# Attention probabilities divided by their sums in place on ScalarE, instead of dividing the output, in a hybrid decoder layer

## The chip, the core and the metric

The kernel runs on one core of a Trainium2 chip. TensorE multiplies matrices and transposes through PSUM; VectorE and ScalarE work on tiles in SBUF and PSUM; GpSimd does elementwise work and starts some transfers; SyncE starts most transfers. Each of these engines takes its instructions in the order in which the program gives them, and they meet at semaphores. The metric is the device time of one execution in microseconds (us). 6 us are about 1% of it.

## The reference, cut to what matters

One layer: a projection feeds eight heads of block-sparse attention (at 512 tokens and blocks of 256 each query sees its own block and all earlier ones, so it is causal attention with a bias by distance) and eight heads of a gated recurrence in chunks; both go through one output projection, and an MLP follows. The change is in the softmax.

```python
        l_own = jnp.einsum('bhqd,bhkd->bhqk', qc, k_own).astype(jnp.float32) * scale
        l_own = l_own + rel_bias[:, rel_bucket(d_own)]
        ...
        logits = jnp.concatenate(
            [l_own, l_sel.reshape(B, H, MOBA_QCHUNK, kk * MOBA_BLOCK)], axis=-1)
        p = jax.nn.softmax(logits, axis=-1)
        ...
        return (jnp.einsum('bhqk,bhkd->bhqd', p_own, v_own)
                + jnp.einsum('bhqnk,bhqnkd->bhqd', p_sel, v_sel))
```

## The kernel before, in words

Every matrix product in float32 is done as three products of rounded halves (`mm3`: high by high, high by low, low by high), or as one slow float32 product. The layer is written as generators ("streams"): `projections`, `chunks`, `inverse` and `scan` (the recurrence), `scores` and `values` (the attention), `finish_o`, `weights_out`, `output` and others. A class `Weave` runs them against a clock of TensorE's work: a stream yields a delay or the name of a mark, and the stream of lowest rank whose time has come writes its next piece of code. So the delays, in the tables `WAIT` (by kind of step) and `SINGLE` (for the n-th step of a kind), set TensorE's order: where a stream waits, units of the projections (one `mm3` of 512 columns, three matmuls `ps_mm<-hT...`) fill the gap. The order on the other engines is set by the framework's scheduler up to the MLP; in the MLP it is the order of the code.

Heads go in four pairs p. `scores` makes for each pair four row blocks q = 3, 2, 1, 0 of 128 queries, 128(q+1) keys wide: six matmuls from `pt` into two PSUM banks `ps_a` (one for each head; the tag "a" has three banks), then for each head an addition of the bias with the row's minimum on VectorE (L708, out `L`, `mins`), and the exponential with its sum on ScalarE (L710, out `L`, `sums`). `values` transposes the rows, a block of 128 keys at a time (`ident,L`, eight for k = 0), ScalarE copies them to `ph` (L736), and `product` multiplies them by the values (`ph,V`) into a bank `po`. At the end of a pair the reciprocal of the eight columns of sums is taken (L713), spread by ScalarE over 512 columns (`R`, L715), transposed by TensorE into a further bank (`ident,R`), copied out by ScalarE (`t`, L762) and multiplied into the output by VectorE (L766), which is then split into `ma_h` and `ma_l`.

Meanwhile the recurrence runs on the same engines: `uap` and `UT` are ScalarE's copies between two small products of the inverse (L815, L828), `kB` and `LWQ` follow, and then eight steps of the scan, each with a copy `vn` on ScalarE (L887) between TensorE's `S,LWQ` and `vn,kdec`. The scan's output of each tile (`ot`) is transposed, multiplied by the gate `zs` (`om`, L933) and split into `mg_h`, `mg_l`. The output projection `output` needs `mg_h`, `mg_l` and its weights `wo_h`, `wo_l`, cast on ScalarE (L142) and VectorE (L143) from loads `wo_raw` that share two slots with the last input weights `w_raw`.

Of the kernel before, what the change touches and what calls it, by code (L numbers as in the profile page):

```python
# [16 lines left out]
DRAM = bass.MemoryType.DRAM  # L17
EPS = 1e-6

WAIT = {'h': 1.7, 'conv_k': 5.5, 'k': 5.19, 'conv_q': 6.15, 'q': 2.1, 'conv_v': 11.0, 'v': 6.02, 'z': 2.87, 'ab': 0.1, 'g': 11.93, 'scalars': 4.76, 'r_in': 0.65, 'r_out': 4.45, 'kk': 2.71, 'kk_out': 14.43, 'gl': 3.13, 'qk': 3.88, 'va': 0.83, 'a': 5.81, 'row': 1.38, 'rows': 5.12, 'pv': 1.54, 'att': 1.17, 'inverse': 1.23, 'merge': 11.0, 'p1': 2.8, 'p2': 1.7, 'w': 2.33, 'vn': 1.0, 'state': 1.21, 'o_in': 3.96, 'o': 3.73, 'wo': 0.97, 'wo_out': 17.6, 'normed3': 7.6, 'normed': 11.21, 'n': 1.7, 'up': 1.9, 'sums': 2.64, 'turned': 0.5, 'pv0': 1.53}  # L20

SINGLE = {('h', 0): 0.05, ('inverse', 6): 2.02, ('state', 6): 3.71, ('row', 5): 0.98, ('inverse', 18): 0.05, ('inverse', 25): 0.05, ('vn', 7): 0.05, ('pv', 2): 0.1, ('h', 1): 0.05, ('turned', 0): 0.9, ('conv_k', 0): 4.12, ('normed', 0): 10.21, ('wo', 1): 1.97, ('conv_q', 0): 8.0, ('inverse', 16): 1.63, ('state', 1): 1.57, ('row', 6): 0.38, ('conv_v', 1): 8.5, ('conv_q', 2): 7.0, ('conv_k', 1): 5.1, ('o_in', 1): 4.36, ('kk', 2): 2.03, ('h', 2): 0.85, ('rows', 2): 6.66, ('vn', 1): 0.75, ('pv', 4): 2.77, ('inverse', 0): 0.61, ('rows', 0): 5.52, ('pv', 6): 2.0, ('rows', 4): 0.1, ('conv_v', 0): 14.3, ('kk_out', 0): 11.93, ('gl', 0): 5.63, ('inverse', 27): 0.23, ('row', 12): 2.48, ('state', 0): 0.21}

RANK = {'chunks': 1, 'inverse': 3, 'scan': 3, 'scores': 5, 'values': 5, 'finish_o': 2, 'take': 4}
LEAD = {'chunks': 0, 'inverse': 100, 'scan': 100, 'scores': 0, 'values': 100, 'finish_o': 0, 'take': 200, 'take_a': 100}
# [60 lines left out]
def layer(ctx, tc, nc, x, w_in, w_v, w_ab, w_out, w_up, w_down, conv_w, a_log, dt_bias, gdn_norm_w, rel_bias,  # L86
# [588 lines left out]

    rows_of, sums_of = {}, {}


    def scores():
        for p in range(4):
            yield f"a{p}"
            if p:
                yield f"turned{p - 1}"
            T = [pts[p][:, i] for i in range(4)]
            Es = []
            for hh in range(2):
                E = at.tile([128, 512], FT, name="E")  # L690
                nc.sync.dma_start(E, bass.AP(tensor=d_e.tensor, offset=d_e.offset + 640 * (2 * p + hh), ap=[[1, 128], [1, 512]]))
                Es.append(E)
            Ls = [at.tile([128, 1280], FT, name="L") for _ in range(2)]
            mins = at.tile([128, 4, 2], FT, name="mins")
            sums = at.tile([128, 4, 2], FT, name="sums")
            for q in (3, 2, 1, 0):
                w = 128 * q + 128
                qs = slice(128 * q, 128 * q + 128)
                s = [bank("a") for _ in range(2)]
                for n, (i, j) in enumerate(((0, 2), (0, 3), (1, 2))):  # L700
                    for hh in range(2):
                        hs = slice(64 * hh, 64 * hh + 64)
# [15 lines left out]
    def values():  # L720
        for p in range(4):
# [646 lines left out]
    rs = {}  # L1368
# [165 lines left out]
```

## Time and profile before

| | |
|---|---|
| median of three runs | 633.07 us (632.63 to 636.78) |
| the profiled execution | 636.12 us |
| its span, first to last instruction | 634.2 us |
| busy: TensorE, VectorE, ScalarE, GpSimd | 622.9, 443.7, 359.4, 157.9 us |
| granted TensorE clock, mean | 0.998 |

The profile is of one execution. Matmuls overlap: one of 512 columns is listed with 0.39 us, and the next starts 0.23 us behind it, so what a group of matmuls costs is read from its start to the start of the next one. An idle time in brackets stands ahead of the instruction that waited, with the instruction that released it.

### The profile page before, as it was taken

To read this page: it belongs to the slowest core of one execution; us is meant where nothing else is said; L and a number is where in the kernel's file an instruction comes from. 1 tells how busy PE (TensorE), PEld (TensorE's weight loads), DVE (VectorE), ACT (ScalarE), POOL (GpSimd) and SP (SyncE) were. 2 spreads that over 40 slices of the span, in tenths; PEclk is the share of its full clock that TensorE was granted. 3 is DMA by queue.
4 is the path that set the end of the run, shared out by engine and by line. 5 is a ranking of instruction groups with operands and counts; after the bars stand their busy time and mean duration, and the time that the engine had idled before them with its cause. 6 is when DMAs were issued, how large, how long until landed. Compare 5 with 4: busy or idle time off the path is not lost.

```text
span 634.2 us, 11129 instructions
## 1 busy us (share of the span) xinstructions
PE 622.9 (98%) x4359; PEld 524.1 (83%) x4359; DVE 443.7 (70%) x635; ACT 359.4 (57%) x610; POOL 157.9 (25%) x197
## 2 busy tenths in 40 slices
PE   8999999999999999999999999999999999999995
PEld 6877777877876777688998999999998888888884
DVE  4456667599724464658665678878789888887776
ACT  6366586254387548654225586566765656665661
POOL 4346555500234343004212311111130320000001
PEclk9999999999999999999999999999999999999999
DMA  7222332422731112563488899999999999867503
GB/s 247 78 90 83 84 109 76 128 88 71 186 94 52 36 35 82 188 229 132 162 336 233 159 276 268 228 241 286 270 264 340 310 291 285 270 213 283 198 1 132
DMA packets 60629, 113.16 MB, mean 178 GB/s; under 512 B 15734, under 2 KB 35321, under 8 KB 60194
## 3 DMA queue, kind: packets, MB, share of 16 engines
q1 hardware_dynamic: 42876, 83.09, 37.8%
q0 software_dynamic: 17696, 29.36, 22.2%
q8 instruction: 34, 0.56, 0.3%
q14 instruction: 17, 0.14, 0.1%
q10 hardware_dynamic: 6, 0.00, 0.0%
HBM read 106.65 MB, written 35.15 MB: 224 GB/s over the span
## 4 chain that ended last, share of the span: by engine, by line
PE 91%; DVE 3%; DMA 2%; ACT 2%; POOL 1%; issue 0%; POOLq 0%; DVEq 0%; SPq 0%; ACTq 0%
PE ps_mm L97 46%; PE ps_g L97 26%; PE ps_a L97 16%; PE ps_a L101 2%; PE ps_g L101 1%; DMA wo_raw<-in_w_out 1%; DMA xx<-in_x 1%; DVE conv L412 1%; DMA w_raw<-in_w_in 0%; DVE wo_l L143 0%; POOL w_lo L155 0%; POOL oss L192 0%; DVE hT_l L131 0%; POOL by L192 0%; DVE xs L249 0%
## 5 line engine op out<-in xcount | busy, mean ns | idle before, releaser
L130 ACT CAST wdh<-wd 128x1024 fp32r<-128x1024 f32 x53 | 55.9, 1054 | 51.4 <-PE ps_mm L97 22.6
L131 DVE TENSOR_TENSOR u_l<-w,u_h 128x1024 fp32r<-128x1024 f32 x46 | 56.2, 1224 | 37.3 <-ACT u_h L130 37.1
L131 DVE TENSOR_TENSOR wdl<-wd,wdh 128x1024 fp32r<-128x1024 f32 x53 | 64.9, 1224 | 22.2 <-ACT wdh L130 22.1
L130 ACT CAST u_h<-w 128x1024 fp32r<-128x1024 f32 x46 | 47.9, 1046 | 56.8 <-DVE w L1177 15.6
L97 PE MATMUL ps_mm<-hT_h,w_hi 128*128 128x512 f32 (+1 forms) x192 | 79.4, 413 | 0.0
L97 PE MATMUL ps_mm<-hT_l,w_hi 128*128 128x512 f32 (+1 forms) x192 | 74.6, 388 | 0.3 <-DVE hT_l L131 0.3
L97 PE MATMUL ps_mm<-hT_h,w_lo 128*128 128x512 f32 (+1 forms) x192 | 74.5, 388 | 0.0
L155 POOL TENSOR_TENSOR w_lo<-w_raw,w_hi 128x512 fp32r<-128x512 f32 x40 | 51.8, 1297 | 77.2 <-ACT w_hi L154 67.4
L1210 POOL DMA_DIRECT2D d_T<-in_w_down x32 | 33.0, 1033 | 143.8 <-DMA d_T<-in_w_down 82.4
L154 ACT CAST w_hi<-w_raw 128x512 fp32r<-128x512 f32 x56 | 34.6, 620 | 52.9 <-PE ps_mm L97 17.5
L97 PEld LDWEIGHTS ps_mm<-hT_h,w_hi 128*128 128x128 f32 x192 | 37.1, 193 | 11.3 <-issue 4.8
L97 PE MATMUL ps_mm<-wdh,u_h 128*128 128x512 f32 x116 | 45.2, 390 | 0.0
L97 PE MATMUL ps_mm<-wdl,u_h 128*128 128x512 f32 x116 | 45.1, 389 | 0.0
L97 PE MATMUL ps_mm<-wdh,u_l 128*128 128x512 f32 x116 | 45.1, 389 | 0.0
L97 PEld LDWEIGHTS ps_mm<-hT_h,w_lo 128*128 128x128 f32 x192 | 37.2, 194 | 7.5
L97 PEld LDWEIGHTS ps_mm<-hT_l,w_hi 128*128 128x128 f32 x192 | 37.3, 194 | 6.0 <-DVE hT_l L131 0.6
L412 DVE SCALAR_TENSOR_TENSOR conv<-ps_mm,cw,conv 128x511 f32<-128x511 f32 (+2 forms) x36 | 26.8, 745 | 11.3 <-ACT conv L409 11.0
L131 DVE TENSOR_TENSOR u_l<-f,u_h 128x1024 fp32r<-128x1024 f32 x28 | 34.1, 1217 | 0.0
L708 DVE CUSTOM_DVE_ANT_0 L<-ps_a,E 128x512 f32<-128x512 f32 (+3 forms) x32 | 14.4, 489 | 23.9 <-PE ps_a L97 23.7
L97 PE MATMUL ps_g<-wdh,u_h 128*128 128x512 f32 x80 | 31.1, 389 | 0.0
L97 PE MATMUL ps_g<-wdl,u_h 128*128 128x512 f32 x80 | 31.1, 389 | 0.0
L97 PE MATMUL ps_g<-wdh,u_l 128*128 128x512 f32 x80 | 31.1, 389 | 0.0
(452 smaller groups left out, 1761.3 us busy)
## 6 DMA issues: line engine op xcount, KB each, us to landing
d_T<-in_w_down POOLq DMA_DIRECT2D x48, 512.0 KB, 11.6
wd<-d_T SPq DMA_DIRECT2D x32, 512.0 KB, 6.2
w<-in_w_up SPq DMA_DIRECT2D x28, 512.0 KB, 8.0
wd<-in_w_down SPq DMA_DIRECT2D x24, 512.0 KB, 7.7
w_raw<-in_w_in SPq DMA_DIRECT2D x46, 256.0 KB, 2.7
wo_raw<-in_w_out SPq DMA_DIRECT2D x16, 256.0 KB, 3.4
d_T<-d_T POOLq DMA_DIRECT2D x8, 512.0 KB, 12.7
xx<-in_x SPq DMA_DIRECT2D x4, 512.0 KB, 6.4
```

Of the source, the lines that this page charges most:

```text
L97: nc.tensor.matmul(o, l, r, **kw)
L101: nc.tensor.transpose(o, i, ident[:k, :k])
L130: nc.scalar.copy(hi, src)
L131: tt(lo, src, f32(hi), op=OP.subtract)
L154: nc.scalar.copy(hi, raw)
L155: (sub or tt)(lo, raw, f32(hi), op=OP.subtract)
L412: stt(c[:, s:], p[:, :512 - s], cw[:, ft, j:j + 1], c[:, s:], op0=OP.mult, op1=OP.add)
L708: nc.vector.tensor_tensor_reduce(out=l, in0=s[hh][:, :w], in1=Es[hh][:, w - 1::-1], scale=1.0, scalar=3e38, op0=OP.add, op1=OP.min, accum_ ...
L1210: nc.gpsimd.dma_start(d_T[t][k], block(b, second)[k], accum_op=OP.add, max_dma_last_dim=1024)
```

## The change

The reciprocal is taken for each row block, of the two columns of sums that belong to it. Then both heads' rows are multiplied by it where they lie in `L`, on ScalarE: a Copy with a scale that differs by partition (the list `BY_SCALAR` names all four pairs; the branch for VectorE isn't taken). What `values` transposes is then already divided. The spread sums, their transposes, the copy and the product of the output go, and `ma_h`, `ma_l` are split straight from the bank `po`. Nothing of the loop over pairs is new: a row's scaling comes ahead of the mark `row`, on which `values` waits.

Two values of `WAIT` and some twenty of `SINGLE` change, so TensorE's order changes: `a` (the delay from a pair's keys to its scores) from 5.81 to 4.65, `ab` from 0.1 to 0.08. In `SINGLE`, among others, ('pv', 4) goes from 2.77 to 1.77, ('row', 4), ('row', 10), ('row', 11), ('row', 14), ('rows', 13), ('pv0', 0), ('a', 1) and ('o_in', 0) are new, ('row', 6), ('row', 12), ('gl', 0) and ('vn', 7) go.

```diff
--- before.py
+++ after.py
@@ -17,9 +17,9 @@
 DRAM = bass.MemoryType.DRAM
 EPS = 1e-6
 
-WAIT = {'h': 1.7, 'conv_k': 5.5, 'k': 5.19, 'conv_q': 6.15, 'q': 2.1, 'conv_v': 11.0, 'v': 6.02, 'z': 2.87, 'ab': 0.1, 'g': 11.93, 'scalars': 4.76, 'r_in': 0.65, 'r_out': 4.45, 'kk': 2.71, 'kk_out': 14.43, 'gl': 3.13, 'qk': 3.88, 'va': 0.83, 'a': 5.81, 'row': 1.38, 'rows': 5.12, 'pv': 1.54, 'att': 1.17, 'inverse': 1.23, 'merge': 11.0, 'p1': 2.8, 'p2': 1.7, 'w': 2.33, 'vn': 1.0, 'state': 1.21, 'o_in': 3.96, 'o': 3.73, 'wo': 0.97, 'wo_out': 17.6, 'normed3': 7.6, 'normed': 11.21, 'n': 1.7, 'up': 1.9, 'sums': 2.64, 'turned': 0.5, 'pv0': 1.53}
-
...
+WAIT = {'h': 1.7, 'conv_k': 5.5, 'k': 5.19, 'conv_q': 6.15, 'q': 2.1, 'conv_v': 11.0, 'v': 6.02, 'z': 2.87, 'ab': 0.08, 'g': 11.93, 'scalars': 4.76, 'r_in': 0.65, 'r_out': 4.45, 'kk': 2.71, 'kk_out': 14.43, 'gl': 3.13, 'qk': 3.88, 'va': 0.83, 'a': 4.65, 'row': 1.38, 'rows': 5.12, 'pv': 1.54, 'att': 1.17, 'inverse': 1.23, 'merge': 11.0, 'p1': 2.8, 'p2': 1.7, 'w': 2.33, 'vn': 1.0, 'state': 1.21, 'o_in': 3.96, 'o': 3.73, 'wo': 0.97, 'wo_out': 17.6, 'normed3': 7.6, 'normed': 11.21, 'n': 1.7, 'up': 1.9, 'sums': 2.64, 'turned': 0.5, 'pv0': 1.53}
+
...
 
 RANK = {'chunks': 1, 'inverse': 3, 'scan': 3, 'scores': 5, 'values': 5, 'finish_o': 2, 'take': 4}
 LEAD = {'chunks': 0, 'inverse': 100, 'scan': 100, 'scores': 0, 'values': 100, 'finish_o': 0, 'take': 200, 'take_a': 100}
@@ -27,6 +27,7 @@
 AT_X = (3, 5)
 START = (5.5, 9.7, 18.5, 13.8, 30, 15.0)
 ORDER = "k0 q0 x0 k1 q1 q2 y0 k2 k3 z0 q3 x1 w0 v0 v1 v2 v3 y1 x2 y2 x3 y3 z1 z2 z3"
+BY_SCALAR = (0, 1, 2, 3)
 LO_DVE = (26, 40)
 V_BANKS = "mm mm a g"
 
@@ -675,8 +676,7 @@
 
 
 
-
-    rows_of, sums_of = {}, {}
+    rows_of = {}
 
 
     def scores():
@@ -708,12 +708,15 @@
                     nc.vector.tensor_tensor_reduce(out=l, in0=s[hh][:, :w], in1=Es[hh][:, w - 1::-1], scale=1.0, scalar=3e38,
                                                    op0=OP.add, op1=OP.min, accum_out=mins[:, q, hh:hh + 1])
                     act(l, l, AF.Exp, bias=mins[:, q, hh:hh + 1], scale=-1.0, accum_out=sums[:, q, hh:hh + 1])
+                nc.vector.reciprocal(sums[:, q], sums[:, q])
+                for hh in range(2):
+                    l = rows_of[p, hh, q]
+                    if p in BY_SCALAR:
+                        act(l, l, AF.Copy, scale=sums[:, q, hh:hh + 1])
+                    else:
+                        nc.vector.tensor_scalar(l, l, sums[:, q, hh:hh + 1], None, op0=OP.mult)
                 yield wait["row"]
                 mark(f"row{p}{q}", wait["rows"])
-            nc.vector.reciprocal(sums, sums)
-            sums_of[p] = at.tile([128, 512], FT, name="R8", bufs=1)
-            nc.scalar.copy(sums_of[p].rearrange("p (q h e) -> p q h e", q=4, h=2), sums[:, :, :, None].to_broadcast([128, 4, 2, 64]))
-            mark(f"sums{p}", wait["sums"])
 
 
 
@@ -754,17 +757,9 @@
                     N = block(0)
                 P = N
             mark(f"turned{p}", wait["turned"])
-            yield f"sums{p}"
-            rb = bank("a")
-            for q in range(4):
-                transpose(rb[:, 128 * q:128 * q + 128], sums_of[p][:, 128 * q:128 * q + 128])
-            rs = at.tile([128, 512], FT, name="t2")
-            nc.scalar.copy(rs, rb)
             yield wait["pv0"]
             product(0, P)
-            mx = at.tile([128, 512], FT, name="t2")
-            tt(mx, po, rs, op=OP.mult)
-            split(mx_h[0][:, p], mx_l[0][:, p], mx)
+            split(mx_h[0][:, p], mx_l[0][:, p], po)
             mark(f"att{p}", wait["att"])
```

The order of the built programs shows what moves. The lines are those of each file, so L97 and L101 of before are L98 and L102 now, L736 is L739, and the scaling is L715. On TensorE, at the end of the second pair (p = 1), before:

```order
L97 MATMUL ps_a<-ph,V 64x384 x2
L101 MATMUL ps_a<-ident,L 128x128 x8
L97 MATMUL ps_g<-UT,kB 64x64 x16
L101 MATMUL ps_a<-ident,R_2025 128x128 x4
L97 MATMUL ps_a<-pt 128x512 x6
L97 MATMUL ps_g<-UT,kB 64x64 x16
L97 MATMUL ps_a<-ph,V 64x512 x2
```

The same place now:

```order
L98 MATMUL ps_a<-ph,V 64x384 x2
L102 MATMUL ps_a<-ident,L 128x128 x8
L98 MATMUL ps_g<-UT,kB 64x64 x16
L98 MATMUL ps_a<-ph,V 64x512 x2
L98 MATMUL ps_a<-pt 128x512 x6
L98 MATMUL ps_mm<-hT_h_82,w_hi 128x512
L98 MATMUL ps_mm<-hT_l_84,w_hi 128x512
```

The transposes of the sums are gone, and the last product of the pair stands in their place, ahead of the third pair's first scores. On ScalarE, the same pair's scores and values up to the copy `uap`, before:

```order
L710 ACTIVATE L,sums<-L,mins 128x512 x2
L736 COPY ph<-ps_a 128x256
L710 ACTIVATE L,sums<-L,mins 128x384
L154 CAST w_hi<-w_raw 128x512
L710 ACTIVATE L,sums<-L,mins 128x384
L710 ACTIVATE L,sums<-L,mins 128x256 x2
L664 ACTIVATE pt<-ps_mm 128x512
L710 ACTIVATE L,sums<-L,mins 128x128 x2
L154 CAST w_hi<-w_raw 128x512
L130 CAST pt<-ps_mm 128x512
L715 COPY R_2025<-sums 128x512
L736 COPY ph<-ps_a 128x512
```

And now:

```order
L710 ACTIVATE L,sums<-L,mins 128x512 x2
L715 ACTIVATE L<-L,sums 128x512 x2
L155 CAST w_hi<-w_raw 128x512
L739 COPY ph<-ps_a 128x256
L710 ACTIVATE L,sums<-L,mins 128x384 x2
L710 ACTIVATE L,sums<-L,mins 128x256 x2
L715 ACTIVATE L<-L,sums 128x384 x2
L715 ACTIVATE L<-L,sums 128x256
L155 CAST w_hi<-w_raw 128x512
L715 ACTIVATE L<-L,sums 128x256
L131 CAST pt<-ps_mm 128x512
L665 ACTIVATE pt<-ps_mm 128x512
```

Six scalings have come in ahead of the copies `ph` and `uap`, and the spreading copy `R` has gone. On ScalarE, around the start of the output projection, before:

```order
L736 COPY ph<-ps_a 128x384 x2
L142 CAST wo_h<-wo_raw 128x512 x2
L478 ACTIVATE zs<-ps_mm 128x512
L480 ACTIVATE t_3076<-zs 128x512
L736 COPY ph<-ps_a 128x512
L142 CAST wo_h<-wo_raw 128x512
L736 COPY ph<-ps_a 128x512
L142 CAST wo_h<-wo_raw 128x512
L130 CAST mg_h<-om 128x4x128
```

And now:

```order
L739 COPY ph<-ps_a 128x384
L143 CAST wo_h<-wo_raw 128x512
L739 COPY ph<-ps_a 128x384
L143 CAST wo_h<-wo_raw 128x512
L479 ACTIVATE zs<-ps_mm 128x512
L481 ACTIVATE t_3075<-zs 128x512
L739 COPY ph<-ps_a 128x512
L143 CAST wo_h<-wo_raw 128x512
L739 COPY ph<-ps_a 128x512
L143 CAST wo_h<-wo_raw 128x512
L131 CAST mg_h<-om 128x4x128
```

Counted from the first, eight casts of output weights stand ahead of `mg_h` before and nine now, and each copy `ph` of this last pair has one or two more casts ahead of it.

## Rows read from the trace of the kernel before

**Rows 1.** The page: span, and busy us (share of the span) xinstructions by engine.

```profile
span 634.2 us, 11129 instructions
...
PE 622.9 (98%) x4359; PEld 524.1 (83%) x4359; DVE 443.7 (70%) x635; ACT 359.4 (57%) x610; POOL 157.9 (25%) x197
```

**Rows 2.** Stretches: length, then busy PE, PEld, DVE, ACT, POOL; clock, DMA.

```profile
175.00:195.00 20.00, 19.75 (x409) 14.09 (x407) 5.73 (x20) 15.99 (x40) 8.02 (x10) 1.00 0.25 76
```

**Rows 3.** TensorE in time order, four places: start us, us, line, operation [idle <-releaser].

```profile
142.24 0.66 PE L101 MATMUL ps_a<-ident,R 128*128 128x128 f32 x4 [0.29 <-ACT ph L736]
142.66 0.48 PE L97 MATMUL ps_mm<-hT_h,w_hi 128*128 128x512 f32 x1
...
190.45 0.66 PE L101 MATMUL ps_a<-ident,R 128*128 128x128 f32 x4
191.04 0.50 PE L97 MATMUL ps_a<-pt 64*128 64x512 f32 x1
...
192.68 0.69 PE L97 MATMUL ps_g<-UT,kB 64*64 64x64 f32 x32
...
219.48 0.66 PE L101 MATMUL ps_a<-ident,R 128*128 128x128 f32 x4
219.89 0.48 PE L97 MATMUL ps_mm<-hT_h,w_hi 128*128 128x512 f32 x1
...
259.31 0.66 PE L101 MATMUL ps_g<-ident,ot 128*128 128x128 f32 x4 [0.40 <-DVE om L933]
259.80 0.60 PE L101 MATMUL ps_a<-ident,R 128*128 128x128 f32 x4
260.33 1.08 PE L97 MATMUL ps_a<-ph,V 128*64 128x512 f32 x4
```

**Rows 4.** TensorE in order of time, second pair of heads.

```profile
172.51 0.97 PE L97 MATMUL ps_a<-pt 64*128 64x512 f32 x6
...
176.39 0.44 PE L101 MATMUL ps_a<-ident,L 128*128 128x128 f32 x2
...
185.44 2.21 PE L97 MATMUL ps_g<-UT,uap 32*32 32x32 f32 x128
...
193.30 1.08 PE L97 MATMUL ps_a<-ph,V 128*64 128x512 f32 x4
```

**Rows 5.** VectorE's groups by line and shape: busy us, mean ns | idle before.

```profile
L766 DVE TENSOR_TENSOR t<-ps_a,t 128x512 f32<-128x512 f32 x4 | 2.7, 687 | 1.8 <-PE ps_a L97 1.8
...
L713 DVE RECIPROCAL sums<-sums 128x8 f32<-128x8 f32 x4 | 0.8, 200 | 0.2
```

**Rows 6.** ScalarE's groups by line and shape, as Rows 5.

```profile
L710 ACT ACTIVATE L<-L,mins 128x512 f32<-128x512 f32 x8 | 5.7, 718 | 6.5 <-DVE mins L708 6.5
...
L710 ACT ACTIVATE L<-L,mins 128x384 f32<-128x384 f32 x8 | 4.9, 613 | 0.9 <-DVE mins L708 0.9
...
L710 ACT ACTIVATE L<-L,mins 128x128 f32<-128x128 f32 x8 | 3.1, 397 | 0.2 <-DVE mins L708 0.2
...
L715 ACT COPY R<-sums 128x512 f32<-128x512 f32 x4 | 2.5, 618 | 0.6 <-DVE sums L713 0.6
```

**Rows 7.** ScalarE in order of time, second pair of heads.

```profile
175.59 0.18 ACT L710 ACTIVATION_READ_ACCUMULATOR L<-L,mins 128x1 f32 x1
...
183.73 2.38 ACT L815 COPY uap<-ps_g 32x512 f32<-32x512 f32 x4
...
189.50 1.08 ACT L736 COPY ph<-ps_a 128x512 f32<-128x512 f32 x2 [0.21 <-PE ps_a L101]
```

**Rows 8.** TensorE, the first matmul of the output projection.

```profile
261.43 0.50 PE L97 MATMUL ps_mm<-wo_h,mg_h 128*128 128x512 f32 x1
```

**Rows 9.** ScalarE in order of time, around the output projection's start.

```profile
260.24 0.62 ACT L142 CAST wo_h<-wo_raw 128x512 fp32r<-128x512 f32 x1 [0.35 <-DMA wo_raw<-in_w_out]
260.77 0.61 ACT L130 CAST mg_h<-om 128x512 fp32r<-128x512 f32 x1
...
262.68 0.62 ACT L142 CAST wo_h<-wo_raw 128x512 fp32r<-128x512 f32 x1 [0.81 <-DMA wo_raw<-in_w_out]
```

More of the change, by code (lines that the diff above doesn't have):

```diff
@@ L22 @@
-SINGLE = {('h', 0): 0.05, ('inverse', 6): 2.02, ('state', 6): 3.71, ('row', 5): 0.98, ('inverse', 18): 0.05, ('inverse', 25): 0.05, ('vn', 7): 0.05, ('pv', 2): 0.1, ('h', 1): 0.05, ('turned', 0): 0.9, ('conv_k', 0): 4.12, ('normed', 0): 10.21, ('wo', 1): 1.97, ('conv_q', 0): 8.0, ('inverse', 16): 1.63, ('state', 1): 1.57, ('row', 6): 0.38, ('conv_v', 1): 8.5, ('conv_q', 2): 7.0, ('conv_k', 1): 5.1, ('o_in', 1): 4.36, ('kk', 2): 2.03, ('h', 2): 0.85, ('rows', 2): 6.66, ('vn', 1): 0.75, ('pv', 4): 2.77, ('inverse', 0): 0.61, ('rows', 0): 5.52, ('pv', 6): 2.0, ('rows', 4): 0.1, ('conv_v', 0): 14.3, ('kk_out', 0): 11.93, ('gl', 0): 5.63, ('inverse', 27): 0.23, ('row', 12): 2.48, ('state', 0): 0.21}
+WAIT = {'h': 1.7, 'conv_k': 5.5, 'k': 5.19, 'conv_q': 6.15, 'q': 2.1, 'conv_v': 11.0, 'v': 6.02, 'z': 2.87, 'ab': 0.08, 'g': 11.93, 'scalars': 4.76, 'r_in': 0.65, 'r_out': 4.45, 'kk': 2.71, 'kk_out': 14.43, 'gl': 3.13, 'qk': 3.88, 'va': 0.83, 'a': 4.65, 'row': 1.38, 'rows': 5.12, 'pv': 1.54, 'att': 1.17, 'inverse': 1.23, 'merge': 11.0, 'p1': 2.8, 'p2': 1.7, 'w': 2.33, 'vn': 1.0, 'state': 1.21, 'o_in': 3.96, 'o': 3.73, 'wo': 0.97, 'wo_out': 17.6, 'normed3': 7.6, 'normed': 11.21, 'n': 1.7, 'up': 1.9, 'sums': 2.64, 'turned': 0.5, 'pv0': 1.53}
@@ new lines @@
+SINGLE = {('h', 0): 0.05, ('inverse', 6): 2.02, ('state', 6): 3.71, ('row', 5): 0.98, ('inverse', 25): 0.05, ('pv', 2): 0.1, ('h', 1): 0.05, ('turned', 0): 0.9, ('conv_k', 0): 4.12, ('normed', 0): 10.21, ('wo', 1): 1.97, ('conv_q', 0): 8.0, ('inverse', 16): 1.63, ('state', 1): 1.57, ('conv_v', 1): 8.5, ('conv_q', 2): 7.0, ('conv_k', 1): 5.1, ('o_in', 1): 4.36, ('kk', 2): 2.03, ('h', 2): 0.85, ('rows', 2): 6.66, ('vn', 1): 0.75, ('pv', 4): 1.77, ('inverse', 0): 0.61, ('rows', 0): 5.52, ('pv', 6): 2.0, ('rows', 4): 0.1, ('conv_v', 0): 14.3, ('kk_out', 0): 11.93, ('inverse', 27): 0.23, ('pv0', 0): 0.53, ('att', 2): 1.57, ('row', 14): 3.88, ('o_in', 0): 2.96, ('row', 4): 2.48, ('a', 1): 5.41, ('inverse', 3): 0.23, ('row', 10): 1.79, ('vn', 2): 1.4, ('rows', 13): 10.12, ('inverse', 4): 2.23, ('inverse', 20): 2.23, ('row', 11): 2.38}
```

## Prediction

> **What bounds the kernel now.** I read the page's busy times first, then the busy times by stretch, then the instructions of the engines in order of time around the changed steps. TensorE is busy for 622.9 us of a span of 634.2, ScalarE for 359.4 [rows 1]. So the end is set by TensorE's row of instructions, and an edit counts by what it takes out of that row or by the waits it puts into it. The stretches say where a wait could arise: from 175 to 195 us, in the scores and values of the second pair of heads, TensorE is busy for 19.75 of 20 us and ScalarE for 15.99 [rows 2]. There ScalarE has 4 us to spare, the least in the attention. Everything behind 262 us is the output projection and the MLP; the change puts nothing in there, and I let a shift at 262 us pass to the end one for one, since none of TensorE's waits in the view of waits lies behind that point.
>
> **What is removed.** Per pair: four transposes of the spread sums (`ident,R`), the copy `t` of their result out of PSUM, the spreading copy `R` (L715), and VectorE's product L766. Only the transposes stand in TensorE's row. Their cost is the time from their start to the next start, with the wait that hangs on them [rows 3]:
> - pair 0: 142.24 to 142.66 is 0.42, and 0.29 of waiting for a PSUM bank before it: 0.71.
> - pair 1: 190.45 to 191.04 is 0.59. Behind it the six score matmuls take from 191.04 to 192.68, 1.64 us, where six of the same shape took about 0.95 elsewhere (0.97 at 172.51 [rows 4]): the second of their banks was held by the turned sums, until ScalarE had copied them. That is 0.69 more, 1.28 in all.
> - pair 2: 219.48 to 219.89, 0.41. Pair 3: 259.80 to 260.33, 0.53.
> Sum 2.9 us. The wait of 0.40 for `om` at 259.31 [rows 3] is another matter and comes with the end of the stage, below. VectorE and ScalarE lose their removed pieces off the path, which gives nothing by itself. Nothing of the sums' turning is left, so this term has little doubt: 2.5 (the switches between kinds of matmul stay as they are, some tenths in all) to 3.1.
>
> **What is added.** 16 reciprocals of two columns on VectorE instead of four of eight; one of eight took 0.200 us [rows 5], and I take the same for two. That is 2.4 us more on VectorE, and the four products that go took 2.7 [rows 5]: nothing. But each waits for the exponentials of both heads and holds up the next row's `L` behind it, for about as long as one exponential.
> On ScalarE 32 scalings by a per-partition operand. No such operation on these tiles is in the trace; the nearest rows are the exponentials L710 on the same tiles, 0.72, 0.61 and 0.40 us for 512, 384 and 128 columns (so 0.50 for 256, midway), and the plain copy L715 at 0.62 for 512 columns [rows 6]. Neighbours on ScalarE overlap by about 0.09, so I take 0.63, 0.52, 0.41, 0.31; twice the sum is 3.7 us per pair, 15 us in all, against 4 x (0.5 + 0.5) removed. ScalarE goes to about 370 us of 634 and is no bound on average. The price is in its queue, since it works in order.
>
> **Pair 1, where ScalarE has the least room.** Three waits may arise:
> - First transposes `ident,L x2`. In the trace they start 3.88 us behind the first score matmul (172.51, 176.39 [rows 4]); the exponential of the second head is read out at 175.59 + 0.18 [rows 7]. The new order puts one unit of projection more (0.69) between them: 4.57. Needed now: 175.77 less 172.51 is 3.26, plus reciprocal 0.24, plus two scalings 1.26, plus a handover of 0.1: 4.86. A wait of 0.3.
> - `UT,uap` starts at 185.44 [rows 4]; ScalarE's copies `uap` begin at 183.73 and take 2.38 for four [rows 7], so the first half (half of 2.38, 1.19) is there at 184.92, 0.5 early. Ahead of them the queue gains 3.1 us of scalings (widths 512, 384, 256) and the first reciprocal's 0.24, loses 0.5 of the copy `R`, and has about 1.5 us of gaps to swallow: 1.3 later. Less the 0.5 of slack and the 0.3 already waited: 0.5.
> - `ph,V` of 512 columns comes at 193.30 in the trace [rows 4], long after its operand `ph` (189.50 + 1.08 [rows 7]). Now it takes the place of the transposed sums at 190.45, while two more scalings (0.6) stand ahead of that copy: about 190.6 + 1.7 against 190.45 + 0.8: 1.0.
> Sum 1.8. Below: 0.7, if the scalings run like plain copies and the gaps swallow them. Above: 2.4. I take 1.5, as ScalarE's 4 us of slack here against an added net 2.6 say that most but not all arrives.
>
> **Scan and pairs 2 and 3.** ScalarE's copies `vn` and `ot` have TensorE's next step behind them, with one or two projection units of cover (0.7 to 1.6 us). Scalings of pairs 2 and 3 stand ahead of some of them (four of 0.4 to 0.6 each in a row). Between 0 and 1.0; I take 0.3, since in rows ahead of the scan two units cover more than two scalings. The moved units themselves (four more ahead of the scan's second step, five fewer behind its end) are the same work in another place: 0.
>
> **The end of the stage.** In the trace the first output matmul starts at 261.43 [rows 8]. Its operand `mg_h` is cast from 260.77, 0.53 behind the eighth cast of the loaded output weights at 260.24, which waited for its DMA; the ninth came at 262.68 and waited 0.81 for its own [rows 9]. In the new order nine of these casts stand ahead of `mg_h`, and one more ahead of each `ph` copy before it. TensorE would arrive 2.9 + 0.4 earlier (the wait for `om` has two more pieces of work to hide behind) and 1.8 later by the two terms above, at about 259.9. If the loads kept to their clock, the cast of `mg_h` would begin at 263.2, 2.4 later than now, and the output at 263.9: a wait of 4.0. They don't quite: their slots are given free by the last input weights, and the projection units that use these come earlier in the new order, by some 3 us of units (five of 0.69 that now stand ahead of the scan's end). So the wait here is between 0 and 4.0; I take 1.3, what is left if the loads come nearly 3 us earlier.
>
> **Sum.** -2.9 - 0.4 + 1.5 + 0.3 + 1.3 = -0.2. The profiled execution took 636.12, with 1.9 us around its span; its time would go to 635.9. The runs shown have a median of 633.07 and lie between 632.63 and 636.78, so the profiled one lies above their median. On the median: 632.9. One per cent, 6.3 us, is about what a measurement of this kernel can tell from no change; by that this is none.
>
> **Rivals.**
> - The queue has room. ScalarE's gaps swallow the scalings, the loads come early enough, and all of 2.9 + 0.4 arrives: 629.8. For it speaks that a one-core kernel with a ScalarE share of 57% leaves 43% free; against it the three places above, where the order is fixed and the gap is not where the work is.
> - The output weights rule. The ninth cast keeps its clock of 262.68 [rows 9] and so sets the first output matmul: then whatever was gained before is swallowed, and the end moves by the 2.4 us by which `mg_h` is later: 635.5, slower than before. It costs against before as soon as the ninth load lands less than 2.4 us earlier than now. For it: both casts shown wait for their DMA, so it is the loads that set their pace. Against it: the slots' chain starts with the projections, which are ahead.
> - ScalarE is too full in all four pairs: each pays pair 1's upper 2.4 and the end its 4.0: 4 x 2.4 + 4.0 - 3.3 = +10.3, 643.4. Only pair 1 has such a stretch; small chance.
> The Trainium skill has a rule against the change: its page "ScalarE: Activation LUTs", section "Rules for kernel authors", sends multiplications to VectorE and not to ScalarE. No row here shows VectorE cheaper on such a tile (its two-operand product took 0.69 [rows 5], against 0.62 for ScalarE's copy [rows 6]). By that rule the terms of ScalarE's queue, 3.1, would go and the sum would be the first rival's.
> That the change doesn't do what it says has no room: the transposes are gone from TensorE's order, and no other instruction took their place.
>
> **Chances.** The forecast, with its own range of 631.2 to 634.5: 0.45. The first rival 0.28, the second 0.22, the third 0.03; 0.02 is left for a gain of more than 1% that I can't name. The range reaches to both of the nearer rivals, with some tenths for the spread of a median: 629.5 to 636. Faster by over 1% (under 626.7) 0.02, within 1% 0.94, slower by over 1% (above 639.4) 0.04.
>
> **What the new profile would show.** TensorE's busy time down by about 2 us and no `ident,R` on `ps_a`; ScalarE's up by 10. Under TensorE's waits: `ident,L` on the new scalings, `uap` or `ph` on ScalarE near 185 to 192 us, `wo_h,mg_h` on the cast L131 (of `mg`) near 260. If the waits near 176 to 192 us are missing, the scalings cost less than I took; if the one near 260 is over 2 us, the second rival holds. The prediction is wrong if TensorE's row gets waits in the MLP, or if the scan's steps stretch with each pair.

## The result, and the profile after

The changed kernel takes 636.65 us (median of 19 executions, 635.28 to 641.84) against 633.38 of the kernel before (19 executions): a ratio of 1.0051, 95% interval 1.0038 to 1.0063, so 2.4 to 4.0 us slower. The forecast was 632.9 in a range of 629.5 to 636.0. By its bound of 1% the change makes no difference, as forecast, but the sign is plainly that of a loss, and the time lies above the range. The interval is 0.25% wide, so far less than the forecast's 1% can be told from no change here.

The profiled execution after has nearly the span of the one before. Its page:

```profile
span 634.4 us, 11122 instructions
...
PE 621.1 (98%) x4343; PEld 521.6 (82%) x4343; DVE 442.9 (70%) x643; ACT 369.3 (58%) x634; POOL 159.2 (25%) x197
```

Against [rows 1] TensorE has lost 1.8 us of work and ScalarE gained 9.9, as expected. But the two executions did not start alike. TensorE in order of time near the start, before:

```profile
14.04 0.41 PE L97 MATMUL ps_mm<-hT_h,w_lo 128*128 128x256 f32 x1
14.25 0.41 PE L97 MATMUL ps_mm<-hT_h,w_hi 128*128 128x256 f32 x1
...
22.09 0.40 PE L97 MATMUL ps_g<-hT_h,abw 128*32 128x512 f32 x1
```

and after:

```profile
14.02 0.28 PE L98 MATMUL ps_mm<-hT_h,w_lo 128*128 128x256 f32 x1
14.14 0.28 PE L98 MATMUL ps_mm<-hT_h,w_hi 128*128 128x256 f32 x1
...
19.83 0.40 PE L98 MATMUL ps_g<-hT_h,abw 128*32 128x512 f32 x1
```

Such matmuls start 0.21 us apart up to 17.45 us before and up to 13.14 after, and 0.12 apart behind that. The view's clock column reads 1.00 from 10 to 18 us in both profiles. But in e10 below it reads 0.50 there, the lower level of 1.2 GHz, and the same matmuls start 0.21 apart too. So the clock rose later in the execution before. By this, and by 0.5 of earlier waits, the first matmul of `abw`, the same instruction in both, starts 2.26 us later before, for no reason of the change. From it to the first output matmul it is 239.34 us before (22.09 to 261.43 [rows 8]) and 241.77 after (19.83 to 261.60, below). So with equal starts TensorE loses 2.4 us, and between these two places. (In the runs below too they differ: in e9 these matmuls start 0.12 apart from 11.4 us on, in e10 from 18.1.)

TensorE's waits in the profile after (line waited for, and the releaser: us in total, times, longest); those that stand unchanged in the start are left out:

```profile
PE ps_g L98 <- ACT vn L882: 1.2, 1, 1.2
...
PE ps_g L98 <- POOL kB L831: 0.8, 1, 0.8
...
PE ps_g L102 <- DVE om L928: 0.6, 1, 0.6
PE ps_g L98 <- ACT uap L810: 0.3, 1, 0.3
PE ps_mm L98 <- ACT mg_h L131: 0.3, 1, 0.3
```

And TensorE in order of time, where these waits and the stretched groups stand:

```profile
174.50 0.66 PE L102 MATMUL ps_a<-ident,L 128*128 128x128 f32 x2
174.91 0.48 PE L98 MATMUL ps_mm<-hT_h,w_hi 128*128 128x512 f32 x1
...
183.24 0.22 PE L98 MATMUL ps_g<-UT,uap 32*32 32x32 f32 x2 [0.18 <-issue]
183.79 2.66 PE L98 MATMUL ps_g<-UT,uap 32*32 32x32 f32 x126 [0.34 <-ACT uap L810]
186.38 1.30 PE L98 MATMUL ps_a<-ph,V 128*64 128x256 f32 x8
...
189.36 1.56 PE L98 MATMUL ps_a<-ph,V 128*64 128x512 f32 x4
190.85 0.96 PE L98 MATMUL ps_a<-pt 64*128 64x512 f32 x6
191.75 0.50 PE L98 MATMUL ps_mm<-hT_h,w_hi 128*128 128x512 f32 x1
...
200.82 0.69 PE L98 MATMUL ps_g<-UT,kB 64*64 64x64 f32 x32 [0.81 <-POOL kB L831]
...
238.17 0.68 PE L98 MATMUL ps_g<-vn,kdec 64*64 64x64 f32 x16 [1.20 <-ACT vn L882]
...
254.61 2.12 PE L98 MATMUL ps_a<-ph,V 128*64 128x256 f32 x8
256.66 1.09 PE L102 MATMUL ps_a<-ident,L 128*128 128x128 f32 x8
...
259.61 0.66 PE L102 MATMUL ps_g<-ident,ot 128*128 128x128 f32 x4 [0.55 <-DVE om L928]
...
261.60 0.50 PE L98 MATMUL ps_mm<-wo_h,mg_h 128*128 128x512 f32 x1 [0.32 <-ACT mg_h L131]
```

The same groups before, where [rows 3] and [rows 4] do not show where they end:

```profile
187.58 1.30 PE L97 MATMUL ps_a<-ph,V 128*64 128x256 f32 x8
...
194.31 0.79 PE L97 MATMUL ps_a<-pt 64*128 64x384 f32 x6
...
254.22 0.65 PE L97 MATMUL ps_a<-ph,V 128*64 128x256 f32 x4
...
255.71 0.87 PE L97 MATMUL ps_a<-ph,V 128*64 128x384 f32 x4
```

(The instructions behind the last two start at 254.80 and 256.50. After, the two groups follow each other from 254.61 and are listed as one.)

No `ident,R` is left, and the six score matmuls at 190.85 take 0.90 again, not the 1.64 of [rows 3]. Where the largest wait comes from is read from ScalarE's row:

```profile
235.61 0.60 ACT L710 ACTIVATE L<-L,mins 128x384 f32<-128x384 f32 x1
236.11 0.18 ACT L710 ACTIVATION_READ_ACCUMULATOR L<-L,mins 128x1 f32 x1
236.53 1.12 ACT L715 ACTIVATE L<-L,sums 128x384 f32<-128x384 f32 x2 [0.23 <-DVE sums L711]
237.56 0.56 ACT L882 COPY vn<-ps_g 64x512 f32<-64x512 f32 x1
```

TensorE had given `vn`'s operand long before (its last `S,LWQ` ended at 234.83). The copy stands behind two scalings, and these behind the reciprocal that waits for the second exponential: 0.23 + 1.12 in front of it, and TensorE waits 1.20. The wait for `kB` at 200.82 is one engine further off. ScalarE and then GpSimd:

```profile
195.35 1.33 ACT L715 ACTIVATE L<-L,sums 128x512 f32<-128x512 f32 x2
...
197.78 0.61 ACT L155 CAST w_hi<-w_raw 128x512 fp32r<-128x512 f32 x1
```

```profile
198.47 1.30 POOL L156 TENSOR_TENSOR w_lo<-w_raw,w_hi 128x512 fp32r<-128x512 f32 x1 [2.81 <-ACT w_hi L155]
199.72 1.05 POOL L831 TENSOR_TENSOR kB<-kdec,kbe 128x512 f32<-128x512 f32 x1
```

GpSimd idles for a cast of weights that ScalarE does behind its exponentials and scalings, and only then makes `kB`. From 195 to 205 us ScalarE had 1.9 us of gaps before (first fence); after (second) it has 0.4 left:

```profile
195.00:205.00 10.00, 9.86 (x167) 7.76 (x165) 4.91 (x19) 8.10 (x22) 4.19 (x4) 1.00 0.18 56
```

```profile
195.00:205.00 10.00, 9.19 (x149) 7.17 (x148) 2.88 (x16) 9.62 (x26) 4.00 (x4) 1.00 0.09 30
```

The forecast had looked for ScalarE's fullest stretch in the order of before, at 175 to 195 us [rows 2]. Even there it was not quite the fullest: from 178 to 198 us ScalarE was busy for 16.90 of 20 us. In the new order the stretch that decides lies behind it, in the scan.

### The profile page after: what moved, and what is told of

Its sections match the earlier page's. It is cut to its first block, busy times and chain, and to the rows that moved or that the text cites. A ratio compares the mean times of both kernels' runs of the same rounds, so it can differ in the third digit from the quotient of the medians.

```text
span 634.4 us, 11122 instructions
## 1 busy us (share of the span) xinstructions
PE 621.1 (98%) x4343; PEld 521.6 (82%) x4343; DVE 442.9 (70%) x643; ACT 369.3 (58%) x634; POOL 159.2 (25%) x197
## 4 chain that ended last, share of the span: by engine, by line
PE 86%; ACT 5%; DVE 4%; DMA 3%; POOL 2%; issue 1%; POOLq 0%; DVEq 0%; ACTq 0%
PE ps_mm L98 42%; PE ps_g L98 25%; PE ps_a L98 15%; DMA wo_raw<-in_w_out 2%; PE ps_a L102 2%; PE ps_g L102 1%; ACT L L710 1%; DVE conv L413 1%; ACT L L715 1%; DMA xx<-in_x 1%; POOL w_lo L156 1%; POOL by L193 1%; ACT wo_h L143 0%; DVE wo_l L144 0%; DVE xs L250 0%
## 5 line engine op out<-in xcount | busy, mean ns | idle before, releaser
L98 PE MATMUL ps_mm<-hT_h,w_hi 128*128 128x512 f32 (+1 forms) x192 | 78.7, 410 | 0.0
L98 PE MATMUL ps_mm<-hT_l,w_hi 128*128 128x512 f32 (+1 forms) x192 | 73.8, 384 | 0.1
L98 PE MATMUL ps_mm<-hT_h,w_lo 128*128 128x512 f32 (+1 forms) x192 | 73.7, 384 | 0.0
L98 PEld LDWEIGHTS ps_mm<-hT_h,w_hi 128*128 128x128 f32 x192 | 36.5, 190 | 10.9 <-issue 4.3
L98 PE MATMUL ps_mm<-wdh,u_h 128*128 128x512 f32 x116 | 45.2, 390 | 0.0
L98 PE MATMUL ps_mm<-wdl,u_h 128*128 128x512 f32 x116 | 45.1, 389 | 0.0
L98 PE MATMUL ps_mm<-wdh,u_l 128*128 128x512 f32 x116 | 45.1, 389 | 0.0
L98 PEld LDWEIGHTS ps_mm<-hT_h,w_lo 128*128 128x128 f32 x192 | 36.4, 189 | 7.5
L98 PEld LDWEIGHTS ps_mm<-hT_l,w_hi 128*128 128x128 f32 x192 | 36.6, 191 | 5.8 <-DVE hT_l L132 0.4
L98 PE MATMUL ps_g<-wdh,u_h 128*128 128x512 f32 x80 | 31.1, 389 | 0.0
L98 PE MATMUL ps_g<-wdl,u_h 128*128 128x512 f32 x80 | 31.1, 389 | 0.0
L98 PE MATMUL ps_g<-wdh,u_l 128*128 128x512 f32 x80 | 31.1, 389 | 0.0
L1404 POOL TENSOR_TENSOR s<-s,mhalf 128x1 f32<-128x1 f32 x4 | 2.2, 552 | 109.1 <-DVE s L1403 109.1
```

The source lines that it names most:

```text
L98: nc.tensor.matmul(o, l, r, **kw)
L1404: nc.gpsimd.tensor_tensor(s1, s1, mhalf[:, :1], op=OP.pow)
```

## The experiments

Two kinds of base are used: the kernel after, and one with "kept order", in which TensorE's instructions are those of before in their order, less the four groups of `ident,R`. In the traces of each base TensorE's instructions are the same in the same order, so the same instruction can be compared from run to run. Ratios are to the kernel before on the same chip (its median there was 633.7 to 635.2).

**The change and the delays, each alone.** e1: after with the tables `WAIT` and `SINGLE` of before. e2: before with those of after.

> The change with the kernel before's delays. Theory A (ScalarE's queue: the scalings stand ahead of copies that TensorE waits for; in the trace after, 0.62 us of UT,uap, 0.81 of UT,kB, 1.20 of vn,kdec and 0.32 of wo_h,mg_h) has new waits of the same sum, 2 to 4 us, at other places, and a time of 635 to 638, ratio to before 1.003 to 1.007. Theory B (the new delays order the work worse, the division itself is free) has the removed 2.9 us come through: 630 to 632, ratio 0.995 to 0.998.

> The kernel before, output divided as before, with the delays of after. Theory A: about as before, ratio 0.999 to 1.003, with no wait of TensorE on kB or vn over 0.3 us. Theory B: slower than before by what after lost and by the turned sums that stay, 636 to 639, ratio 1.004 to 1.009.

e1: 644.25, ratio 1.0149 (1.0120 to 1.0177). e2: 644.94, ratio 1.0160 (1.0133 to 1.0186). Both are 9 to 10 us slower, far beyond any theory: since the clock of `Weave` counts the removed transposes, a table that belongs to another code moves units of projection among the steps all along TensorE's order. e2 is not as before, as theory A had it, and shows only that delays do not carry over. Part of it is the clock: behind the start the granted clock stood at the lower level for 10.2 us in e1 and for 6.8 in e2. Neither says what the division costs; that needed the order to be held.

**After with its scalings on VectorE, and with none.**

```diff
-BY_SCALAR = (0, 1, 2, 3)
+BY_SCALAR = ()
```

> After, with the 32 scalings on VectorE and not on ScalarE; nothing else. Theory A: the waits for vn (1.20), uap (0.62) and kB (0.81, by way of a cast of weights on ScalarE) go or shrink under 0.3 each, VectorE's own queue may give back a part; 633.5 to 635.5, 1 to 3 us under after. Theory B: as after, 636 to 637.5.

> After without the 16 reciprocals and the 32 scalings: the probabilities are not divided at all, the output isn't the reference's; the order is that of after. It measures what all of the division costs where it now stands. Theory A: the four waits go, 2.95 us, and with them what each held up: 632.5 to 633.7. If after also lost in places that the trace doesn't show as waits, 630 to 632. Theory B: 635.5 to 637, as after, with waits of the same size left.

e3: 639.9, ratio 1.0087 (1.0062 to 1.0113): the waits for `vn` and `uap` went, but that for `kB` is 1.2, and VectorE's later work brought 1.8 for the recurrence's `S` and 1.1 for `ident,L`; a stop of 1.7 with a fall of the clock, as in e4 below, came too. e4, without reciprocals and scalings: 637.78, ratio 1.0051 (1.0031 to 1.0070), the ratio of after itself. Taken alone that would say the division is free. Its waits say otherwise:

```profile
PE ps_g L102 <- DVE om L921: 2.1, 1, 2.1
PE ps_g L98 <- issue: 1.9, 1, 1.9
```

The waits for `vn`, `kB` and `mg_h` are gone, and two others came. One is a stop within `UT,uap` that no instruction explains. Behind it the granted clock stood at the lower level:

```profile
186.00:193.00 7.00, 6.77 (x85) 4.60 (x86) 0.00 (x0) 2.35 (x4) 0.20 (x1) 0.51 0.01 2
193.00:200.00 7.00, 7.00 (x95) 4.40 (x92) 2.95 (x9) 4.75 (x12) 4.00 (x4) 1.00 0.01 4
```

7 us at about half speed lose some 3.4 us of work. So the stop costs about 5 us in all, an estimate from these rows (1.85 and 3.4), and hides what leaving out the division gave.

**TensorE's order kept.** The code is that of after with the tables of before, and `Weave` is told the time that the transposes took:

```diff
             mark(f"turned{p}", wait["turned"])
+            yield f"sums{p}"
+            weave.now += 4 * 128 * 4 / 2400
             yield wait["pv0"]
             product(0, P)
```

(and the mark `sums` is set at the end of a pair, as before). e5 divides on ScalarE, e6 not at all, e7 on VectorE.

> The change (division by ScalarE, no turned sums) with TensorE's instructions in exactly the order of the kernel before, less the four groups of ident,R. Theory A (the scalings in ScalarE's row hold up copies that TensorE waits for): -2.9 for the removed pieces, +3 to +5 of waits on ScalarE, so 0 to 2 us above before, 633.4 to 635.4 by before's 633.4. Theory B (the division is free, the new order costs): -2.9, 630.5. Theory C (not ScalarE but TensorE's own stream stops, in a wait that the profile puts down to issue, with the granted clock at 1.2 GHz behind it, 1.85 us and 3.4 us in the run without division): a stop of 1.5 us or more at UT,uap wherever ScalarE no longer keeps TensorE there; here ScalarE still does, so as A.

> The same order as the run with kept order, without reciprocals and scalings: nothing is divided, the output isn't the reference's. It measures what is removed by itself. Theories A and B: 2.9 us under before, 630.5, with the waits of before left (om 0.4) and no stop of the clock. Theory C: TensorE comes to UT,uap earlier and stops there for 1.5 to 2.3 us, the clock falls for 3.4 to 6.8 us behind it, and of the 2.9 nothing is left: 632.5 to 635.

> The same order again, with the 32 scalings on VectorE. Theory A: the waits move from ScalarE's row to VectorE's (33 scalings' worth of about 0.3 to 0.6 us ahead of pt, S and om); 1 to 4 us above the run without division. Theory B: as the run without division.

| | median | ratio (95%) |
|---|---|---|
| e6, nothing divided | 631.69 | 0.9968 (0.9947 to 0.9988) |
| e7, VectorE | 636.63 | 1.0045 (1.0027 to 1.0063) |
| e5, ScalarE | 640.81 | 1.0104 (1.0081 to 1.0128) |

This settles the main point. The removal alone brings 2.0 us (0.8 to 3.4). The division costs 4.9 us on VectorE and 9.1 on ScalarE, with one order of TensorE. Theory B falls; theory C falls for e6, whose `UT,uap` does not stop. A was right in kind and too low in size. Counted from the first matmul of `abw`, e5 comes 0.8 us later than e6 ahead of pair 1 (165 us), 2.0 later behind pair 1 (186), 5.9 at the first `vn,kdec` (197), 7.3 at the second (201), 7.5 at the first output matmul and 8.8 at the end. e7 comes 2.0 later already at 165, since it waits 1.6 for `kraw` from VectorE at 84, and 4.1 at the end. e5's waits are spread over the scan and reach into the MLP (the largest; `rb` and `kraw`, which before has too, and 0.9 for `om`, less than e6's, left out):

```profile
PE ps_g L98 <- ACT vn L885: 1.4, 2, 0.9
PE ps_a L102 <- DVE xs L1035: 1.4, 1, 1.4
...
PE ps_a L98 <- DVE ma_l L132: 1.0, 1, 1.0
...
PE ps_g L98 <- ACT LWQ L843: 0.7, 1, 0.7
```

Not all of the 9.1 is waiting. Between the first and second `vn,kdec`, behind three waits of 0.7 to 1.0, e5's granted clock stood at the lower level for 3.4 us:

```profile
205.00:208.50 3.50, 3.38 (x23) 2.71 (x23) 1.22 (x4) 1.28 (x3) 0.00 (x0) 0.51 0.65 164
```

That is the 1.4 by which e5 falls further behind e6 there. In the traces of e6, e7 and e10 the clock stays at the higher level from its last rise, at the start, to TensorE's last matmul.

After, with 1.0051, lies half as far above before as e5, with 1.0104: its own delays win back 3.4 us of the division's price in the old order.

In e6 the 2.0 are less than the 2.9 that the removed pieces take, since the wait for `om` grew from 0.40 [rows 3] to 1.21. TensorE, and ScalarE ahead of it:

```profile
254.75 0.66 PE L102 MATMUL ps_g<-ident,ot 128*128 128x128 f32 x4 [1.21 <-DVE om L924]
```

```profile
251.33 0.62 ACT L143 CAST wo_h<-wo_raw 128x512 fp32r<-128x512 f32 x1 [1.45 <-DMA wo_raw<-in_w_out]
251.85 0.59 ACT L479 ACTIVATE zs<-ps_mm 128x512 f32<-128x512 f32 x1
```

The gate `zs`, which `om` needs, stands in ScalarE's row behind a cast of output weights that waits for its DMA. The 2.9 us by which TensorE comes earlier here thus turn in part into waiting.

**Two rows moved to VectorE in after**: those of 512 columns of pair 2 and of 384 of pair 3.

```diff
-BY_SCALAR = (0, 1, 2, 3)
+BY_VECTOR = ((2, 3), (3, 2))
...
-                    if p in BY_SCALAR:
+                    if (p, q) not in BY_VECTOR:
```

> After, with the scalings of two rows of probabilities on VectorE: those of 512 columns of pair 2, which stand ahead of the cast of weights that kB waits behind, and those of 384 columns of pair 3, which stand ahead of vn. TensorE's order is that of after. Theory A: the waits of 0.81 for kB and 1.20 for vn go, so 1.5 to 2.0 us under after, 634.7 to 635.2, ratio to before 1.002 to 1.003. Theory B and C: the waits stay or others of the same size take their place, 636 to 637.

638.6, ratio 1.0064 (1.0040 to 1.0088): not faster. The wait of 1.20 at `vn,kdec` went, but 1.01 came at the scan's last step, 2.1 at `om`, and `kB` has 1.1. For `kB` the way now leads through VectorE: the two scalings take 1.61 us there, the next row's minimum comes behind them, and ScalarE waits 1.39 for it ahead of the same cast of weights. The cost moves; taking single scalings out of ScalarE's row does not remove it. (This execution also has a fall of the clock for 3.4 us at 187.5, which after's does not have, though TensorE's waits from 170 us up to there are nearly the same, 0.16 and 0.34 here, 0.18 and 0.34 there. Against after it costs 1.3 us, and nothing shows that the edit brought it.)

**Other places for the scalings, TensorE's order kept.** e9: GpSimd. e10: the first head's on ScalarE, the second's on VectorE (`if hh == 0:` in place of the pair's test). e11: ScalarE, a row's scalings behind the next row's exponentials.

> TensorE's order kept as in the kernel before, the 32 scalings on GpSimd (busy for a quarter of the span). Theory A (a scaling costs what its engine's later work is late by): GpSimd has the gaps, but one scaling of 512 columns should take about the 1.05 us of its products of that size, so a row of two comes about 1 us later than on ScalarE: waits at the first transposes ident,L of each pair of 0.5 to 1 us, and the casts of weights behind them; 2 to 5 us above the run without division (631.7), 634 to 637. Theory B (any engine with enough free time hides them): as the run without division, 631 to 632.5.

> Kept order, of each row's two scalings that of the first head on ScalarE and that of the second on VectorE. Theory A: each queue gets half, and the two run side by side, so the delay of what stands behind is less than half of 9.1 and 4.9: 2 to 4 us above the run without division, 633.5 to 635.5, under both kernels that use one engine (640.8 and 636.6). If the cost comes from whichever queue has the less room: as with ScalarE alone, 638 to 641.

> Kept order, all scalings on ScalarE, but a row's scalings are written behind the exponentials of the next row, so that ScalarE does not stand idle for the sums' reciprocals (0.23 to 0.70 us in front of many scalings of after). If this idling is what holds up the copies behind: 2 to 4 us under the run with kept order (640.8), 636.5 to 639. If it is the scalings' own time (15 us in all) that does: 640 to 642, as there.

e9: 651.8, ratio 1.0266 (1.0244 to 1.0288); a scaling of 512 columns takes 1.59 us there, and TensorE waits up to 6.2 us for `R` of the recurrence. e10: 635.68, ratio 1.0013 (0.9993 to 1.0032): as before, 2.8 us above e6, and better than after. Halving each queue's share takes two thirds of the 9.1 away.

e11: 640.45, ratio 1.0089 (1.0062 to 1.0116). It does not test what it was meant to. In the traces TensorE, VectorE, ScalarE and GpSimd do the same instructions in the same order in e11 and e5: the scheduler put the scalings back where they had been. So e11 is e5 measured again, and agrees with it within the intervals. Whether the idling for the reciprocals costs anything was not tried. In e5's trace ScalarE idles for 1.7 us in all ahead of the 32 scalings and is busy with them for 16.2, so their own time is the likelier cause.

e10's largest wait behind the start is at the end of the stage:

```profile
260.82 0.66 PE L102 MATMUL ps_g<-ident,ot 128*128 128x128 f32 x4 [1.95 <-DVE om L931]
```

But e6, without any division, waits 1.21 of this too. Counted from the first `abw`, e10 comes 0.1 us later than e6 at 165 us, 2.0 later at the first `vn,kdec`, 2.6 at the first output matmul and 2.2 at the end. So most of what is left of the price arises in pair 1 and at the scan's start.

**Casts of output weights off ScalarE.** The first eight casts `wo_h` go to GpSimd: e12 in after, e13 in e10, e14 in before. Then only the last three of them: e15 in e10, e16 in after.

```diff
-        nc.scalar.copy(hi, raw)
+        (cast or nc.scalar.copy)(hi, raw)
```

> After, with the first eight casts of output weights (wo_h) on GpSimd and not on ScalarE; TensorE's order is that of after. They wait for their DMA, and on ScalarE everything behind them waits with them. Theory A (the scalings alone are to blame): as after, 636 to 637. Theory D (the loads of output weights reach TensorE through ScalarE's row: by ph of pair 3, 0.7 us, by zs and om, 0.55, by mg_h, 0.32): 1.0 to 1.6 us under after, ratio to before 1.002 to 1.004.

> The kernel with kept order and the scalings split between ScalarE and VectorE, with the same eight casts on GpSimd. Its wait for om was 1.95 us, and in ScalarE's row the activation of z that leads to om stood behind a cast that had waited 1.17 us for its DMA. Theory D: that wait falls under 0.8, and the time to 1.0 to 1.7 us under the split kernel, ratio to before 0.998 to 1.000. Theory A: as the split kernel, 1.0013.

> The kernel before, with the same eight casts on GpSimd. TensorE comes to this place later than without the turned sums, and waits 0.40 for om. Theory D: at most these 0.4 us are won, ratio 0.998 to 1.000; the gain is smaller than that of the split kernel and of after. If the eight casts on GpSimd are worth 1 us here too, they are not what the change ran into.

> The kernel with kept order and split scalings, with only the last three of the first eight casts of output weights on GpSimd; VectorE's order around xs of the MLP is again that of before (with all eight casts moved, two more splits of weights, 0.69 each, stood ahead of xs, and TensorE waited 1.18 there). Theory D: the wait for om (1.95) goes under 0.8 and no wait at 292 us comes in its place, 1.0 to 1.7 us under the split kernel: ratio to before 0.997 to 1.000. If the loads of output weights hold TensorE up anyway, at mg_h, wo_h or further back: as the split kernel, 1.001.

> After, with the same three casts on GpSimd. Theory D: the waits for om, mg_h and ph of pair 3 go (1.5 us), none comes at 296 us: ratio to before 1.002 to 1.003, where after has 1.005. Otherwise 1.004 to 1.005.

e12: 637.25, ratio 1.0035 (1.0015 to 1.0055). e13: 635.69, 1.0011 (0.9995 to 1.0028). e14: 635.73, 1.0011 (0.9996 to 1.0027). e15: 634.27, 1.0003 (0.9987 to 1.0019). e16: 636.77, 1.0037 (1.0020 to 1.0055). In all five the waits for `mg_h` and `om` are under 0.2 us, so they did come through ScalarE's row. But none of the five is faster than its base by more than the intervals: a wait of 0.9 to 1.4 us came in the MLP, at about 290 to 296 us. In e12 to e14 VectorE's order had moved there; in e15 and e16 it had not, and the wait came nonetheless (e15):

```profile
PE ps_a L102 <- DVE xs L1036: 1.4, 1, 1.4
```

There the chain to `xs` stands on ScalarE behind a cast of the MLP's first weights (`wu`), which waits 0.48 for its own DMA. From the first `abw` to the first output matmul e15 takes 1.9 us less than e10, and from there to TensorE's end 2.2 more: what was won at `om` is lost again here. The weights' loads may be the next bound at this end; it was not tried by itself. That TensorE comes early is not needed for it: e5 comes 7.5 us later than e6, and waits the same 1.4 for `xs`, behind a cast of `wu` that waits 0.49 for its DMA. No version that divides is faster than the kernel before; e15 equals it.

## Why the prediction was wrong

- **Bound.** Right: the end is TensorE's row, and the costs came as waits in it (in e5 a fall of the clock too). That a shift at 262 us passes to the end one for one held for the change: from the first output matmul to TensorE's last one it is 366.2 us in both traces. In e1, e2, e5, e11 and e12 to e16 it did not hold: 367.0 to 368.0.
- **Removed pieces, -2.9.** Right in size: 0.29 + 0.42 + 0.59 + 0.41 + 0.53, and 1.64 - 0.90 for the six scores, are 2.98. The 0.4 for `om` was wrong in sign. It was taken as a wait that later work hides. But ScalarE's row and the loads in it set when it ends, and it grew to 0.55 in after and 1.21 in e6.
- **Price of a scaling.** Right. 0.63 to 0.31 were taken. The groups show 0.71 to 0.40 (us in all, mean ns), of which about 0.09 overlaps with the next instruction: two of 512 columns take 1.33 in a row, and the next starts 0.10 before they end. ScalarE is busy for 9.9 us more, where 10 were forecast.

```profile
L715 ACT ACTIVATE L<-L,sums 128x512 f32<-128x512 f32 x8 | 5.3, 713 | 0.9 <-DVE sums L711 0.9
...
L715 ACT ACTIVATE L<-L,sums 128x128 f32<-128x128 f32 x8 | 2.9, 399 | 0.2 <-DVE sums L711 0.2
```

- **Pair 1, +1.5.** About right, in part by luck: `ident,L` 0.41 against 0.19, 0.2 where 0.3 was forecast; `UT,uap` 3.14 (183.24 to 186.38) against 2.14, 1.0 where 0.5 was forecast; `ph,V` 1.49 against 1.01, 0.5 where 1.0 was. With 0.25 more for the six transposes ahead of `UT,uap` this is 1.95.
- **Scan and pairs 2 and 3, +0.3.** This is the step that failed. It cost 0.81 for `kB` and 1.20 for `vn`, 2.0, above the bound of 1.0. Without the division, in the same order, both waits are gone (e4). "Two units cover more than two scalings" left out that the scalings wait for a reciprocal (0.23) and stand behind the row's two exponentials. The operand of `vn` was there at 234.83 and the copy began at 237.56, 2.7 us later; TensorE's cover, a row's scores and two units, was 2.2 (234.76 to 236.97). And `kB` was not among the terms: its wait runs through GpSimd's row, by a cast of weights on ScalarE. In before's order such waits are more: 9.1 us in e5 against e6, with the clock's fall in it.
- **The end of the stage, +1.3 (less 0.4).** About right: `om` 0.15 more, `mg_h` 0.32, and `ph,V` of pair 3, 2.05 (254.61 to 256.66) against 1.37 before, together 1.15. The second rival's mechanism was there, with the loads behind it, but `mg_h`, its way, took 0.32 of the 2.4 that it priced.
- **Sum.** 1.95 + 2.0 + 1.15 and 0.15 at pair 0's last product are 5.25; less 2.98 this is +2.3, where the forecast had -0.2. It accounts for nearly all of the 2.4 us between the two traces at equal starts. The medians differ by 3.3 (2.4 to 4.0). What the rest is stays open: one profiled execution of each kernel does not show it.
- **Rivals.** The first, that the queue has room, is excluded by e5 and e6. The second's 635.5 was nearest to the time, by luck: most of the loss arose ahead of the place that it named. The third, all four pairs full, was dismissed at 0.03. For before's order e5 comes near it in time (640.8, 643.4 forecast), but not by its mechanism: pair 0 costs 0.8, the end of the stage gives some back, and the most is lost at the scan's start. The Trainium skill's rule in "ScalarE: Activation LUTs", "Rules for kernel authors", multiplications on VectorE, was weighed against rows of other operations alone. In e7 VectorE's scalings took 0.28 us for 128 columns and 0.48 for 512 where nothing disturbed them, and that kernel is 4.2 us faster than e5: the rule held there. In the order made for ScalarE e3 is slower than after, 1.0087 against 1.0051, but the stop and the fall of the clock in its trace keep it from deciding. By the rule as I used it, the terms of ScalarE's queue would have gone to nothing; VectorE's queue cost 4.9 us (e7).

## What to carry to other kernels

An operation moved to an engine with time to spare is paid for in the order of that engine's row: price what stands behind it in the order of after, through the third engine too, and not the engine's mean share. To measure such a change where delays set the order, hold the bottleneck's order fixed and take the work out; the kernels with another order (e1, e2) told nothing of it. Compare the built orders before reading a result: e11's edit had changed none. A wait whose end something else sets (here loads, by casts in ScalarE's row) can grow by what is won ahead of it.

## What the runs showed of the hardware

A scaling of 512 columns on VectorE took 0.48 us alone, but over 1.2 us where it met a GpSimd product. In e7 two of them took 1.67, of which the second is 0.48; GpSimd's row there:

```profile
193.69 1.67 DVE L717 TENSOR_SCALAR L<-L,sums 128x512 f32<-128x512 f32 x2
```

```profile
193.63 1.05 POOL L835 TENSOR_TENSOR kdec<-kdec,kde 128x512 f32<-128x512 f32 x1
```

The first began 0.06 us behind the GpSimd product, and ended at about 194.9, 0.2 behind the product's end. The Trainium skill, "SBUF — State Buffer", "SBUF: two separate sides", has a VectorE operation in a 2-port mode and a GpSimd operation share a port pair, which the one that starts first holds for its whole instruction. These rows agree; which mode the scaling ran in, they do not show.

Stops of 1.7 to 2.3 us within `UT,uap`, which the profile puts down to issue, came in e2, e3 and e4, with the granted clock at the lower level behind them. What TensorE's sequencer waits for there was not tried.

The length of a wait alone did not tell whether the clock would fall. Waits of 1.8 to 2.1 us for `om` were followed by no fall in e3, e4, e8 and e10, and by one of 3.4 us in e1. In e5 the clock fell behind several waits of 1.0 at most. In e8 it fell where after's, with nearly the same waits ahead of it, did not. Why was not tried.
